# Modulation vectors with the float32 weight block as stationary operand and two conditioning columns streaming

## The chip, the core and the metric

The kernel runs on one core of a Trainium2 chip: TensorE (PE, with its weight loads PEld), VectorE (DVE), ScalarE (ACT), GpSimd (POOL) and SyncE (SP, which issues the DMAs here). The metric is the time of the kernel on the device in microseconds.

## The reference

One inference step of a backbone of two layers on 128 context tokens and 512 latent tokens, D = 1024. Each layer normalises its input, modulates it, sends it through one wide projection into three mixers (attention A, latent attention B, a bidirectional scan C), gates and merges them, and adds the result back. What the change touches is the modulation: for each of two conditioning vectors (`c_ctx` for context tokens, `c` for latent tokens) and each layer, a product of a vector of 1024 with a 1024 x 3072 matrix, split into shift, scale and gate.

```python
def _modulation(cond, w, b):
    m = jax.nn.silu(cond) @ w + b
    return jnp.split(m, 3, axis=-1)

shift, scale, gate = _modulation(c_ctx[None, None, :], w_mod[l], b_mod[l])
h = _rmsnorm(xp, norm_w[l]) * (1.0 + scale) + shift
out, ak, av, ckv, kr, s_f, s_b = _context_mixer(h, lp)
xp = xp + gate * out
```

The latent tokens go the same way with `c`.

## The kernel before

Features lie on partitions: the state is 8 tiles (`KT`) of 128 features x 640 tokens. Its modulated form `hh`, `hl` is a float32r pair (rounded part and remainder), and so is every weight block: `load_w1` fetches a block of 128 output columns (8 x 128 x 128, 512 KB, in `self.pieces` pieces), ACT rounds a piece into `whi` (L174), DVE or POOL subtracts it for `wlo` (L175), and three products (`hh` by `whi`, `hl` by `whi`, `hh` by `wlo`, L225 to L227, tile `pcm`) stand for one float32 product, in two halves of 320 tokens.

The modulations are 24 blocks of 128 outputs a layer. A block gives a column of 128 values for each of the two conditioning vectors in `modc`.

The first 16 (shift and scale of layer 0) are computed in the opening, by `modulation_first`, from float32 weights as they come (`wraw`, eight buffers): `sc2` (128 x 2, the two conditioning vectors) is stationary, the weights stream, the result is two rows of 128, which ACT copies (`mrow`, L263) and a second small product (L264) turns into two columns of 128. The opening also loads `x0`, sums its squares (`pss`, L311), spreads the reciprocal root over partitions (`prb`, L319), normalises (L326) and modulates into `hh`, `hl` (L163, L164). The first products that read them are the LoRA products (`plo`, L178 to L180, 96 of them), at the start of the scan stage.

The other 32 (8 gates of layer 0, 16 shift and scale blocks of layer 1, 8 gates of layer 1) lie in the scan stages as fillers. There a stream of projections (`c_inproj`, `spill`, `gate`), a Python generator, is played between the steps of the scan (`c_scan`: `sca`, `scb`), `pump(rate)` taking so many `yield`s from it, and after every `every` units `fillers` inserts a modulation. A scheduler with a timeline of its own then settles each engine's order. In these stages `pieces` is 2, and there are two raw buffers (`nraw`, of half a block each) and two `whi` and `wlo` buffers (`nw`), shared by projections and modulations. `modulation` (L241) uses the pair: `sc_t` (128 x 4, also split) is stationary, `whi` and `wlo` stream (L247, L248, 16 products), ACT copies four rows into the zeroed `mrow` (L249), and after a `yield` a float32 product with `mrow` as stationary operand and `sel` streaming (L251) sums and transposes them. The subtraction is given to POOL (`self.G`). The PSUM tile `pmod` comes from the two banks that the projections use.

Of the kernel before, what the change touches and what calls it, by code (L numbers as in the profile page):

```python
# [10 lines left out]
F32 = mybir.dt.float32  # L11
F32R = mybir.dt.float32r
AF = mybir.ActivationFunctionType
ALU = mybir.AluOpType
# [6 lines left out]
KT = 8  # L21
# [44 lines left out]
NR0 = 8  # L66
# [27 lines left out]
def f32(ap):  # L94
    return ap.bitcast(F32)
# [12 lines left out]
class Trunk:  # L108
    def __init__(self, ctx, tc, I, O):
# [5 lines left out]
        V, G = self.V, self.G  # L115
# [3 lines left out]
        self.dr = ctx.enter_context(tc.tile_pool(name="dr", bufs=1, space=DRAM))  # L119


        c = cst.tile([128, 202], F32, tag="small", name="small")
        nc.sync.dma_start(out=c, in_=I["small"])
        self.cT = c[:, 0:16].rearrange("p (k c) -> p k c", c=2)
        self.bmod = c[:, 16:64].rearrange("p (l k) -> p l k", l=DEPTH)
        self.fnw = c[:, 64:72]
        self.ident = c[:, 72:200]
        self.sel = c[:, 200:202]
        self.mrow = cst.tile([128, 128], F32, tag="mrow", name="mrow")
        G.memset(self.mrow, 0.0)  # L130

        self.bones_r = cst.tile([128, 128], F32R, tag="bones", name="bones")
        self.bones = f32(self.bones_r)
        for h in range(2):
            for g in range(2):
# [5 lines left out]
        self.sc2 = sc = cst.tile([128, KT, 2], F32, tag="sc", name="sc")  # L141
        self.S.activation(out=sc, in_=self.cT, func=AF.Tanh, scale=0.5)
        V.scalar_tensor_tensor(out=sc, in0=sc, scalar=1.0, in1=self.cT, op0=ALU.add, op1=ALU.mult)

        self.sc_t = st = cst.tile([128, 2, KT, 4], F32R, tag="sc_t", name="sc_t")
        self.S.mul(out=st[:, 0, :, 0:2], in_=sc, mul=0.5)
        V.scalar_tensor_tensor(out=st[:, 0, :, 2:4], in0=sc, scalar=0.5, in1=f32(st[:, 0, :, 0:2]),
                               op0=ALU.mult, op1=ALU.subtract)
        self.S.copy(out=st[:, 1, :, 0:2], in_=f32(st[:, 0, :, 0:2]))
        self.S.mul(out=st[:, 1, :, 2:4], in_=sc, mul=0.0)  # L150
        dr = self.dr
        self.x1 = dr.tile([KT, 128, T], F32, tag="x1", name="x1")
        self.gsp = [[dr.tile([128, T], F32, tag=f"gsp{b}_{k}", name=f"gsp{b}_{k}") for k in range(KT)] for b in range(3)]
# [84 lines left out]
        return r  # L238


    def modulation(self, l, ct, wp, ps, sub=None, tag="f"):  # L241

        PE, S = self.PE, self.S
        hi, lo = self.load_w1(wp, self.I["wmod"][l, ct], sub=sub)
        pm = ps.tile([128, 512], F32, tag=tag, name="pmod")
        for kt in range(KT):
            PE.matmul(pm[0:4, 0:128], lhsT=self.sc_t[:, 0, kt, :], rhs=hi[:, kt], start=(kt == 0), stop=False)  # L247
            PE.matmul(pm[0:4, 0:128], lhsT=self.sc_t[:, 1, kt, :], rhs=lo[:, kt], start=False, stop=(kt == KT - 1))  # L248
        S.copy(out=self.mrow[0:4], in_=pm[0:4, 0:128])  # L249
        yield  # L250
        PE.matmul(pm[:, 256:258], lhsT=self.mrow, rhs=self.sel, start=True, stop=True)  # L251
        self.V.tensor_scalar(out=self.modc[l][:, ct // KT, ct % KT, :], in0=pm[:, 256:258],  # L252
                             scalar1=self.bmod[:, l, ct:ct + 1], scalar2=None, op0=ALU.add)

    def modulation_first(self, ct, wp, ps, tag):

        raw = wp.tile([128, KT, 128], F32, tag="wr", name="wraw", bufs=NR0)
        self.nc.sync.dma_start(out=raw, in_=self.I["wmod"][0, ct])
        pm = ps.tile([128, 512], F32, tag=tag, name="pmod")
        for kt in range(KT):  # L260
            self.PE.matmul(pm[0:2, 0:128], lhsT=self.sc2[:, kt], rhs=raw[:, kt], start=(kt == 0), stop=(kt == KT - 1))
        row = wp.tile([4, 128], F32, tag="mrow", name="mrow", bufs=2)
        self.S.copy(out=row[0:2], in_=pm[0:2, 0:128])  # L263
        self.PE.matmul(pm[:, 256:258], lhsT=row[0:2], rhs=self.sel[0:2], start=True, stop=True)  # L264
        self.V.tensor_scalar(out=self.modc[0][:, ct // KT, ct % KT, :], in0=pm[:, 256:258], scalar1=0.5,
                             scalar2=self.bmod[:, 0, ct:ct + 1], op0=ALU.mult, op1=ALU.add)


    def layer_vectors(self, l):
# [1066 lines left out]
    def run(self):  # L1336
# [30 lines left out]
        ps = P("psA0", **PSA)  # L1367
        with ExitStack() as ctx:
            wp = pool(ctx, "wp0", 1, side="right")
            op = pool(ctx, "op0", 2, side="right")  # L1370
            xs = op.tile([128, KT, T], F32, tag="xs", name="xs", bufs=1)
            order = [(kt, ct, "g" if kt % 2 else "f") for kt in range(KT) for ct in (kt, KT + kt)]

            for kt, ct, tag in order[:MF]:
                self.modulation_first(ct, wp, ps, tag)
            self.layer_vectors(0)
            for kt in range(KT):
                nc.sync.dma_start(out=xs[:, kt], in_=self.I["x0"][kt])
                self.square(xs[:, kt], kt, op)
            for kt, ct, tag in order[MF:MG]:  # L1380
                self.modulation_first(ct, wp, ps, tag)
            self.normalise(xs, self.token_rstd(self.acc, self.sq, op, ps))
            for kt in range(KT):
                for k, ct, tag in order[MG:]:
                    if k == kt:
                        self.modulation_first(ct, wp, ps, tag)
                self.mod_vectors(0, [kt])
                self.modulate(0, xs, kt, 0, T, op)
        for l in range(DEPTH):
            plan = self.plan = NS(**PLAN[l])  # L1390
            if l:
                ps = P(f"psA{l}", **PSA)
            with ExitStack() as ctx, ExitStack() as ctx_c, ExitStack() as ctx_e:
                wp = pool(ctx, f"wp1{l}", 1)
                st = pool(ctx, f"st1{l}", 2)
# [18 lines left out]
                def fillers(n):  # L1414
                    for _ in range(n):
                        yield from units.pop(0)
                        count[0] += 1
                        while mods and count[0] >= every:
                            count[0] -= every
                            yield from self.modulation(*mods.pop(0), wp, ps, self.G)  # L1420

                def keys(p):

# [15 lines left out]
                def period(p, x):  # L1439

                    z = self.spill(self.silu2, l, W_CZ + p, wp, st, ps, self.zsp[p])
                    if p < 3:
                        def between():
                            yield from z
                            yield from fillers(plan.fb[p])
                        e = yield from prepare(*x, between())
                        yield from fillers(plan.share[p + 1] - plan.fb[p])
                        return e, (yield from keys(p + 2)) if p < 2 else None
                    yield from z
                    yield from fillers(plan.at[0])  # L1450
                    es = yield from self.attention_start(l, pools, wp, st, ps, lambda i: fillers(min(plan.at[i], len(units))))
                    yield from fillers(len(units))
                    for m in mods:
                        yield from self.modulation(*m, wp, ps, self.G)
                    return None, es

                c = self.play(prepare(*self.play(keys(0))))
# [77 lines left out]
def _layout(i):  # L1535
# [22 lines left out]
    def pc(v):  # L1558
# [14 lines left out]
    wo = np.stack([a["w_oa"], a["w_ob"], a["w_oc"]], 1)  # L1573
    r["wo"] = wo.reshape(2, 3, 4, 128, 4, 256).transpose(0, 1, 4, 3, 2, 5)
    r["wout"] = blocks1(a["w_out"])
    sel = np.zeros((128, 2), np.float32)
    sel[0:4] = np.concatenate([np.eye(2), np.eye(2)], 0)
    r["small"] = np.concatenate([
        np.stack([a["c_ctx"], a["c"][0]], -1).reshape(KT, 128, 2).transpose(1, 0, 2).reshape(128, 16),
        a["b_mod"].reshape(2, 24, 128).transpose(2, 0, 1).reshape(128, 48),  # L1580
        a["final_norm_w"].reshape(KT, 128).T, np.eye(128, dtype=np.float32), sel], 1)
    r["kc"] = a["cache_a_k"][0]
    r["vc"] = a["cache_a_v"][0]
    r["ckvc"] = a["cache_b_ckv"][0]
# [35 lines left out]
```

## Time and profile before

| | |
|---|---|
| median of 3 runs | 2349.75 us (2346.33 to 2349.75) |
| the profiled execution | 2358.59 us |
| its span, first to last instruction | 2356.9 us |
| mean granted TensorE clock | 0.934 |
| opening | 0 to about 61 us |
| scan stage of layer 0 | about 52 to 800 us |
| the 32 later modulations, first to last | 104.7 to 1909.3 us |

Busy shares are of the span. The clock is the share of the full 2.4 GHz that was granted; it has two levels, 1.00 and 0.50. A wait is the idle time of an engine before an instruction, with what ended it.

### The profile page before, as it was taken

Reading aid. Unit: us, or ns where it says so; the run is one execution under the profiler, and the core shown is the slowest. Engines: PE = TensorE matmul, PEld = TensorE weight load, DVE = VectorE, ACT = ScalarE, POOL = GpSimd, SP = SyncE. Lnnn points to the kernel's source line nnn. Section 1 sums busy time; section 2 is a strip of 40 time slices with the busy share of each in tenths; the row PEclk is TensorE's granted clock in tenths of the full one; section 3 lists DMA queues with packets and bytes.
Section 4 is the critical chain, followed back from the end, with each engine's and each line's share of the span. In section 5 each row is a group of like instructions: output and inputs, shape, how many; then the busy total and the mean of one; then the engine's idle time right before and its main releaser. Section 6 shows DMA issues by size and latency. Waiting matters only on the chain. (4 is left out here: it accounts for less than half of the span.)

```text
span 2356.9 us, 40407 instructions
## 1 busy us (share of the span) xinstructions
PE 2144.3 (91%) x15380; PEld 2025.6 (86%) x15380; DVE 1603.2 (68%) x3054; ACT 1107.0 (47%) x2462; POOL 694.8 (29%) x769
## 2 busy tenths in 40 slices
PE   8889998999779889999989999999897888999998
PEld 6889998989678777879988999989896877788898
DVE  4667878868544677775748778687774458677673
ACT  4544443444343567662344444443442436677333
POOL 3332536145233311102033143351632341210021
PEclk9999998999789899999989999999996989999999
DMA  6232222222223311125622322222222220110552
GB/s 224 77 100 80 82 75 81 86 90 94 79 75 98 107 36 52 39 76 172 203 64 68 106 73 86 74 71 84 81 82 76 73 95 30 51 46 17 186 183 89
DMA packets 111762, 209.70 MB, mean 89 GB/s; under 512 B 14416, under 2 KB 33488, under 8 KB 111568
## 3 DMA queue, kind: packets, MB, share of 16 engines
q1 hardware_dynamic: 111568, 207.12, 27.6%
q8 instruction: 121, 1.98, 0.3%
q14 instruction: 73, 0.60, 0.1%
HBM read 163.52 MB, written 43.55 MB: 88 GB/s over the span
## 5 line engine op out<-in xcount | busy, mean ns | idle before, releaser
L225 PE MATMUL pcm<-hh,whi 128*128 128x320 f32 x1952 | 636.1, 326 | 16.5 <-ACT xv L378 2.9
L227 PE MATMUL pcm<-hh,wlo 128*128 128x320 f32 x1952 | 627.9, 322 | 11.3 <-DVE wlo L175 11.3
L226 PE MATMUL pcm<-hl,whi 128*128 128x320 f32 x1952 | 625.1, 320 | 0.0
L225 PEld LDWEIGHTS pcm<-hh,whi 128*128 128x128 f32 x1952 | 382.1, 196 | 24.5 <-DVE modc L252 5.0
L227 PEld LDWEIGHTS pcm<-hh,wlo 128*128 128x128 f32 x1952 | 380.9, 195 | 15.1 <-DVE wlo L175 13.9
L226 PEld LDWEIGHTS pcm<-hl,whi 128*128 128x128 f32 x1952 | 381.9, 196 | 1.2
L174 ACT CAST whi<-wraw 128x512 fp32r<-128x512 f32 (+1 forms) x356 | 226.9, 666 | 322.0 <-PE pcm L226 116.8
L175 DVE TENSOR_TENSOR wlo<-wraw,whi 128x512 fp32r<-128x512 f32 (+1 forms) x262 | 220.9, 857 | 78.3 <-ACT whi L174 74.9
L175 POOL TENSOR_TENSOR wlo<-wraw,whi 128x512 fp32r<-128x512 f32 x94 | 124.4, 1337 | 157.4 <-ACT whi L174 152.4
L778 POOL COPY ubd<-VZ 64x128 f32<-64x128 f32 x160 | 65.0, 406 | 354.9 <-ACT VZ L775 324.3
L164 DVE TENSOR_TENSOR pl<-pp,ph 128x512 fp32r<-128x512 f32 x160 | 107.9, 684 | 35.5 <-ACT ph L163 34.7
L958 DVE TENSOR_REDUCE nm<-sc 128x1 f32<-128x640 f32 x128 | 104.2, 818 | 28.7 <-PE sc L955 27.5
L178 PE MATMUL pm<-yh,whi 128*128 128x320 f32 x384 | 121.5, 317 | 2.0 <-DVE OT L992 1.5
L179 PE MATMUL pm<-yl,whi 128*128 128x320 f32 x384 | 121.1, 315 | 0.5 <-DVE yl L167 0.4
L180 PE MATMUL pm<-yh,wlo 128*128 128x320 f32 x384 | 120.8, 315 | 0.7 <-DVE wlo L175 0.7
L163 ACT CAST ph<-pp 128x512 fp32r<-128x512 f32 x160 | 92.1, 585 | 46.5 <-PE pp L970 36.6
L960 ACT ACTIVATE P<-sc,nm 128x640 f32<-128x640 f32 x128 | 101.9, 797 | 17.4 <-DVE nm L958 14.0
L970 PE MATMUL pp<-small,P 128*128 128x128 f32 x640 | 102.0, 284 | 7.3 <-DVE pl L164 2.5
L767 PE MATMUL sca<-VZ,L 128*128 128x64 f32 x640 | 96.5, 296 | 11.1 <-DVE VZ L799 11.1
L767 PEld LDWEIGHTS sca<-VZ,L 128*128 128x128 f32 x640 | 93.8, 217 | 12.8 <-DVE VZ L799 12.3
L970 PEld LDWEIGHTS pp<-small,P 128*128 128x128 f32 x640 | 81.9, 146 | 25.0 <-DVE OT L992 3.9
L613 PE MATMUL pA<-L,BK 128*128 128x128 f32 x640 | 93.1, 290 | 6.3 <-DVE BK L549 3.1
(375 smaller groups left out, 4987.5 us busy)
## 6 DMA issues: line engine op xcount, KB each, us to landing
wraw<-in_win SPq DMA_DIRECT2D x156, 256.0 KB, 3.0
wraw<-in_wg SPq DMA_DIRECT2D x96, 256.0 KB, 3.0
wraw<-in_wmod SPq DMA_DIRECT2D x64, 256.0 KB, 3.1
gsp<-gt SPq DMA_DIRECT2D x48, 320.0 KB, 2.6
gt<-gsp SPq DMA_DIRECT2D x48, 320.0 KB, 3.5
wraw<-in_wo SPq DMA_DIRECT2D x24, 512.0 KB, 4.4
cm<-gsl SPq DMA_DIRECT2D x26, 320.0 KB, 2.7
wraw<-in_wmod SPq DMA_DIRECT2D x16, 512.0 KB, 6.6
```

The lines of the kernel that those rows point to most:

```text
L164: self.V.tensor_tensor(out=lo, in0=src, in1=f32(hi), op=ALU.subtract)
L174: self.S.copy(out=hi[part], in_=raw)
L175: sub.tensor_tensor(out=lo[part], in0=raw, in1=f32(hi[part]), op=ALU.subtract)
L178: self.PE.matmul(out, lhsT=lh, rhs=rh, start=first, stop=False)
L179: self.PE.matmul(out, lhsT=lh, rhs=rl, start=False, stop=False)
L180: self.PE.matmul(out, lhsT=ll, rhs=rh, start=False, stop=last)
L225: PE.matmul(p[0:m, 0:H], lhsT=wh[:, kt], rhs=self.hh[:, kt, rs], start=(kt == 0), stop=False)
L226: PE.matmul(p[0:m, 0:H], lhsT=wh[:, kt], rhs=self.hl[:, kt, rs], start=False, stop=False)
L227: PE.matmul(p[0:m, 0:H], lhsT=wl[:, kt], rhs=self.hh[:, kt, rs], start=False, stop=(kt == KT - 1))
L767: PE.matmul(a4[:, d, h], lhsT=L1[h][:, uu[d]].rearrange("p a s -> p (a s)"), rhs=VZ[h][:, cc[d], :], start=(h == 0 and d == 0), stop=False ...
L958: V.tensor_reduce(out=nm, in_=sc[:, :, 0:H], axis=AX.XY, op=ALU.max, negate=True)
L970: PE.transpose(p[:, qt * 128:(qt + 1) * 128], Ps[qt][:, t * 128:(t + 1) * 128], ident)
```

## The change

One method, `modulation`, replaces both. It streams the two columns of `sc2` against the raw float32 weights as stationary operand: 8 products per block, each of 128 x 128 by 128 x 2, straight into two columns of `pmod`, and DVE adds the bias with a factor 0.5. The rounding, the subtraction, the second stationary operand `sc_t`, the copied row and the second product are gone, with `sel` and `mrow`. There is a `yield` after each piece (two a modulation in the scan stages, before one). The raw buffers are read by PE itself.

```diff
-        self.sel = c[:, 200:202]
-        self.mrow = cst.tile([128, 128], F32, tag="mrow", name="mrow")
-        G.memset(self.mrow, 0.0)
...
-        self.sc_t = st = cst.tile([128, 2, KT, 4], F32R, tag="sc_t", name="sc_t")
-        self.S.mul(out=st[:, 0, :, 0:2], in_=sc, mul=0.5)
-        V.scalar_tensor_tensor(out=st[:, 0, :, 2:4], in0=sc, scalar=0.5, in1=f32(st[:, 0, :, 0:2]),
-                               op0=ALU.mult, op1=ALU.subtract)
-        self.S.copy(out=st[:, 1, :, 0:2], in_=f32(st[:, 0, :, 0:2]))
-        self.S.mul(out=st[:, 1, :, 2:4], in_=sc, mul=0.0)
...
-    def modulation(self, l, ct, wp, ps, sub=None, tag="f"):
-
-        PE, S = self.PE, self.S
-        hi, lo = self.load_w1(wp, self.I["wmod"][l, ct], sub=sub)
+    def modulation(self, l, ct, wp, ps, tag="f"):
+
         pm = ps.tile([128, 512], F32, tag=tag, name="pmod")
-        for kt in range(KT):
-            PE.matmul(pm[0:4, 0:128], lhsT=self.sc_t[:, 0, kt, :], rhs=hi[:, kt], start=(kt == 0), stop=False)
-            PE.matmul(pm[0:4, 0:128], lhsT=self.sc_t[:, 1, kt, :], rhs=lo[:, kt], start=False, stop=(kt == KT - 1))
-        S.copy(out=self.mrow[0:4], in_=pm[0:4, 0:128])
-        yield
-        PE.matmul(pm[:, 256:258], lhsT=self.mrow, rhs=self.sel, start=True, stop=True)
-        self.V.tensor_scalar(out=self.modc[l][:, ct // KT, ct % KT, :], in0=pm[:, 256:258],
-                             scalar1=self.bmod[:, l, ct:ct + 1], scalar2=None, op0=ALU.add)
-
-    def modulation_first(self, ct, wp, ps, tag):
-
-        raw = wp.tile([128, KT, 128], F32, tag="wr", name="wraw", bufs=NR0)
-        self.nc.sync.dma_start(out=raw, in_=self.I["wmod"][0, ct])
-        pm = ps.tile([128, 512], F32, tag=tag, name="pmod")
-        for kt in range(KT):
-            self.PE.matmul(pm[0:2, 0:128], lhsT=self.sc2[:, kt], rhs=raw[:, kt], start=(kt == 0), stop=(kt == KT - 1))
-        row = wp.tile([4, 128], F32, tag="mrow", name="mrow", bufs=2)
-        self.S.copy(out=row[0:2], in_=pm[0:2, 0:128])
-        self.PE.matmul(pm[:, 256:258], lhsT=row[0:2], rhs=self.sel[0:2], start=True, stop=True)
-        self.V.tensor_scalar(out=self.modc[0][:, ct // KT, ct % KT, :], in0=pm[:, 256:258], scalar1=0.5,
-                             scalar2=self.bmod[:, 0, ct:ct + 1], op0=ALU.mult, op1=ALU.add)
+        n = KT // self.pieces
+        for i in range(0, KT, n):
+            raw = wp.tile([128, n, 128], F32, tag="wr", name="wraw", bufs=self.nraw)
+            self.nc.sync.dma_start(out=raw, in_=self.I["wmod"][l, ct][:, i:i + n])
+            for k in range(n):
+                self.PE.matmul(pm[:, 0:2], lhsT=raw[:, k], rhs=self.sc2[:, i + k], start=(i + k == 0),
+                               stop=(i + k == KT - 1))
+            yield
+        self.V.tensor_scalar(out=self.modc[l][:, ct // KT, ct % KT, :], in0=pm[:, 0:2], scalar1=0.5,
+                             scalar2=self.bmod[:, l, ct:ct + 1], op0=ALU.mult, op1=ALU.add)
...
+            self.pieces, self.nraw = 1, NR0
...
-                self.modulation_first(ct, wp, ps, tag)
+                self.play(self.modulation(0, ct, wp, ps, tag))
...
-                            yield from self.modulation(*mods.pop(0), wp, ps, self.G)
+                            yield from self.modulation(*mods.pop(0), wp, ps)
```

The built order of PE in the opening, before: the products of a modulation (L261) and the product with its row (L264).

```order
L261 MATMUL pmod<-wraw,sc 2x128 x19
L264 MATMUL pmod<-small,mrow 128x2
L261 MATMUL pmod<-wraw,sc 2x128 x8
L264 MATMUL pmod<-small,mrow 128x2
L261 MATMUL pmod<-wraw,sc 2x128 x8
```

And after, from the start to the first LoRA products.

```order
L239 MATMUL pmod<-sc,wraw 128x2 x82
L288 MATMUL pss<-ones,acc 128x2 x5
L239 MATMUL pmod<-sc,wraw 128x2 x13
L296 MATMUL prb<-small,tr5b 128x128 x5
L239 MATMUL pmod<-sc,wraw 128x2 x33
L168 MATMUL plo<-hh,whi 128x320
L169 MATMUL plo<-hl,whi 128x320
```

All 128 products of the 16 modulations now stand ahead of the LoRA products, with nothing between them but `pss` and `prb`; before, the last of them and the LoRA products alternated.

SP's queue around one modulation of layer 0, before, with the semaphores that each DMA waits for (`DMAHW` of DMAs, `DVE_49` and `Pool_49` of those engines, `PE_49` of TensorE). `wraw` from `in_wmod` is the modulation's weight, from `in_wg` that of the gate block after it.

```order
L173 DMA wraw_7253<-in_wmod 128x512 [waits DMAHW7_49,DMAHW2_49,DVE_49]
L173 DMA wraw_7257<-in_wmod 128x512 [waits DMAHW3_49,DMAHW1_49,DVE_49]
L1253 DMA gsp0_7_95<-gt_7057 128x640 [waits DMAHW4_49,Activation_49]
L173 DMA wraw_7351<-in_wg 128x512 [waits DMAHW5_49,DMAHW2_49,Pool_49]
L173 DMA wraw_7355<-in_wg 128x512 [waits DMAHW6_49,DMAHW3_49,Pool_49]
```

And after, around one.

```order
L237 DMA wraw_7409<-in_wmod 128x512 [waits DMAHW7_49,DVE_49]
L237 DMA wraw_7419<-in_wmod 128x512 [waits DMAHW0_49,DVE_49]
L1230 DMA gsp1_4_93<-gt_7348 128x640 [waits DMAHW3_49,Activation_49]
L163 DMA wraw_7428<-in_wg 128x512 [waits DMAHW4_49,DMAHW1_49,PE_49]
L163 DMA wraw_7432<-in_wg 128x512 [waits DMAHW5_49,DMAHW2_49,PE_49]
```

What releases the next block's buffer has moved from POOL's subtraction to PE's products.

PE's order at the same modulation, after: the end of the gate before it, its own products from the two pieces, and the first products of the gate behind it.

```order
L217 MATMUL pcm_7381<-hh_149,wlo_7339 128x320
L239 MATMUL pmod_7408<-sc_77,wraw_7409 128x2 [waits DMAHW1_49,Activation_49]
L239 MATMUL pmod_7408<-sc_77,wraw_7409 128x2 x3
L239 MATMUL pmod_7408<-sc_77,wraw_7419 128x2 [waits DMAHW2_49]
L239 MATMUL pmod_7408<-sc_77,wraw_7419 128x2 x3
L215 MATMUL pcm_7437<-hh_149,whi_7426 128x320 [waits Activation_49]
```

Here four products of the second piece are all that stands between the first piece's release and the next block, whose `whi_7426` is cast from `wraw_7428`.

## Rows read from the trace of the kernel before

**Rows 1.** The page, part 1: busy us (share) and instructions.
```profile
PE 2144.3 (91%) x15380; PEld 2025.6 (86%) x15380; DVE 1603.2 (68%) x3054; ACT 1107.0 (47%) x2462; POOL 694.8 (29%) x769
```

**Rows 2.** Table by stretch: length, busy us of each engine (instructions), clock, DMA share, GB/s.
```profile
0.00:30.00 30.00, 23.10 (x181) 16.49 (x182) 8.07 (x25) 10.70 (x25) 7.61 (x19) 1.00 0.94 347
```

**Rows 3.** PE's waits, 52 to 850 us: us in total, times, longest.
```profile
PE pmod L248 <- POOL wlo L175: 2.1, 2, 1.7
PE pmod L251 <- ACT mrow L249: 1.9, 2, 1.3
...
PE pcm L225 <- DVE modc L252: 1.6, 1, 1.6
```

**Rows 4.** The modulation's own products in a stretch; PE's timeline around a second product.
```profile
509.50:510.80 1.30, 1.12 (x16) 0.96 (x16) 0.00 (x0) 0.00 (x0) 1.00 0.00 0
...
116.74 0.28 PE L251 MATMUL pmod<-small,mrow 128*128 128x2 f32 x2
...
117.11 0.31 PE L226 MATMUL pcm<-hl,whi 128*128 128x320 f32 x1
```

**Rows 5.** PE's timeline: neighbouring stream products at full clock, then at half.
```profile
60.98 0.31 PE L179 MATMUL plo<-hl,whi 128*128 128x320 f32 x1
61.13 0.31 PE L180 MATMUL plo<-hh,wlo 128*128 128x320 f32 x1
...
113.17 0.47 PE L226 MATMUL pcm<-hl,whi 128*128 128x320 f32 x1
113.43 0.47 PE L227 MATMUL pcm<-hh,wlo 128*128 128x320 f32 x1
```

**Rows 6.** Two columns on a stationary 128*128 block: full clock, durations of one, half clock.
```profile
29.66 1.28 PE L311 MATMUL pss<-ones,acc 128*128 128x2 f32 x10 [1.28 <-DVE acc L308]
...
L311 PE MATMUL pss<-ones,acc x30: 165/251/374, 29.7 to 2346.0; 128*128 128x2 f32 x30
...
1211.38 1.01 PE L311 MATMUL pss<-ones,acc 128*128 128x2 f32 x4 [3.60 <-POOL acc L300]
```

**Rows 7.** Table by stretch, as rows 2: the start, before and after three falls; L681 from 1490.1.
```profile
5.50:8.70 3.20, 3.17 (x16) 1.94 (x17) 0.00 (x0) 0.00 (x0) 0.00 (x0) 1.00 1.01 398
...
1490.10:1493.50 3.40, 3.40 (x75) 3.35 (x72) 1.61 (x4) 0.00 (x0) 0.00 (x0) 1.00 0.79 249
1493.60:1496.90 3.30, 3.30 (x14) 3.30 (x14) 0.28 (x1) 1.52 (x4) 0.58 (x2) 0.50 0.01 3
1503.80:1507.10 3.30, 2.47 (x23) 2.33 (x22) 2.13 (x6) 1.58 (x4) 2.95 (x2) 1.00 0.60 216
1507.20:1514.00 6.80, 5.43 (x22) 5.03 (x21) 3.33 (x8) 3.65 (x12) 5.01 (x6) 0.50 0.23 84
...
510.50:513.90 3.40, 2.00 (x15) 1.73 (x13) 2.59 (x6) 0.85 (x3) 0.78 (x1) 1.00 0.27 104
513.90:517.30 3.40, 3.40 (x15) 3.40 (x14) 2.49 (x3) 1.97 (x3) 1.28 (x1) 0.50 0.42 149
...
L681 PE MATMUL px<-NF,AB 32*32 32x32 f32 x75 | 3.7, 228 | 0.0
```

**Rows 8.** DVE's timeline at the opening's end; POOL's in layer 0's last group norm.
```profile
55.60 1.56 DVE L164 TENSOR_TENSOR hl<-mt,hh 128x640 fp32r<-128x640 f32 x2 [2.62 <-ACT hh L163]
...
771.64 1.30 POOL L175 TENSOR_TENSOR wlo<-wraw,whi 128x512 fp32r<-128x512 f32 x1 [1.17 <-ACT whi L174]
772.89 1.97 POOL L237 TENSOR_TENSOR gsb<-gs,nhalf 128x10 f32<-128x10 f32 x1
```

**Rows 9.** DMA issues (page, part 6), and timelines of SP, ACT and PE.
```profile
wraw<-in_win SPq DMA_DIRECT2D x156, 256.0 KB, 3.0
...
495.62 1.56 SPq L173 DMA_DIRECT2D wraw<-in_wg  x2
...
61.34 1.14 ACT L174 CAST whi<-wraw 128x512 fp32r<-128x512 f32 x2
...
62.01 0.42 PE L225 MATMUL pcm<-hh,whi 128*128 128x320 f32 x1 [0.57 <-ACT whi L174]
...
511.29 0.42 PE L225 MATMUL pcm<-hh,whi 128*128 128x320 f32 x1 [0.58 <-ACT gt L1252]
```

More of the change, by code (lines that the diff above doesn't have):

```diff
@@ L119, in __init__ @@
         self.dr = ctx.enter_context(tc.tile_pool(name="dr", bufs=1, space=DRAM))
-        c = cst.tile([128, 202], F32, tag="small", name="small")
+        c = cst.tile([128, 200], F32, tag="small", name="small")
         nc.sync.dma_start(out=c, in_=I["small"])
@@ L1380, in run @@
             for kt, ct, tag in order[MF:MG]:
-                self.modulation_first(ct, wp, ps, tag)
+                self.play(self.modulation(0, ct, wp, ps, tag))
             self.normalise(xs, self.token_rstd(self.acc, self.sq, op, ps))
@@ L1385, in run @@
                     if k == kt:
-                        self.modulation_first(ct, wp, ps, tag)
+                        self.play(self.modulation(0, ct, wp, ps, tag))
                 self.mod_vectors(0, [kt])
@@ L1453, in period @@
                     for m in mods:
-                        yield from self.modulation(*m, wp, ps, self.G)
+                        yield from self.modulation(*m, wp, ps)
                     return None, es
@@ L1575, in _layout @@
     r["wout"] = blocks1(a["w_out"])
-    sel = np.zeros((128, 2), np.float32)
-    sel[0:4] = np.concatenate([np.eye(2), np.eye(2)], 0)
     r["small"] = np.concatenate([
@@ L1580, in _layout @@
         a["b_mod"].reshape(2, 24, 128).transpose(2, 0, 1).reshape(128, 48),
-        a["final_norm_w"].reshape(KT, 128).T, np.eye(128, dtype=np.float32), sel], 1)
+        a["final_norm_w"].reshape(KT, 128).T, np.eye(128, dtype=np.float32)], 1)
     r["kc"] = a["cache_a_k"][0]
```

## The prediction

> **What bounds the kernel now.** I read the page's busy shares first, then a table by stage, then the list of PE's waits, then the instructions of the modulations alone. TensorE is busy 91% of the span [rows 1]; only in the opening 30 us are the DMA engines the fuller ones, at 0.94 [rows 2]. In the list of PE's waits in the scan stage of layer 0 (52 to 850 us) those on modulations come to 5.6 us: `wlo` from POOL 2.1, `mrow` from ACT 1.9, `modc` 1.6 [rows 3]. So PE time is time of the kernel there; ACT and POOL work is not, unless it holds PE up.
>
> **PE work of the 32 later modulations.** Now: 16 products in float32r take 1.12 us, the last of them some 0.22 after its start, so 60 ns each, 0.96 together [rows 4]. The product with the copied row is two passes: from the first of them (116.74) to the second stream matmul after it (117.11) 0.37 us pass, of which the stream matmul has 0.147 [rows 4, 5], so 0.22. Together 1.18 us. After: 8 float32 products of a 128*128 stationary block with two columns. The trace has this form as L311: ten passes (five matmuls) in 1.28 us, the last one 0.25 long, so 0.112 a pass [rows 6]. That is 16 x 0.112 = 1.79 us, 0.61 more, **+19.5 us** for 32. The Trainium skill (TensorE: Matmul & The Clock Gate, Back-to-back issue gap) gives about 25 ns as the floor for so few columns; by that alone a modulation would take 0.4 us, and this term would be -25 in place of +19.5. The rows decide against it.
>
> **The opening.** Its 16 modulations already use float32 without a split; only the roles change. PE starts at half speed (16 passes in the 3.2 us to 8.7, though the clock column, whose records begin there, reads 1.00) and goes on at full speed (181 by 30 us) [rows 2, 7]. With two streaming columns I expect it to stay at half. What speaks for that: before each fall in rows 7 PE was busy, 3.40 of 3.40 us from 1490.1 with 32*32 matmuls alone, 2.47 of 3.30 from 1503.8 with weight loads for 2.33; the clock then stood at 0.50 (1.2 GHz). At half clock a pass of this form takes 0.213 (four passes in 1.01, the last 0.37 long) [rows 6]. The order puts 82 products ahead of the sums of squares (`pss`): 82 x 0.426 = 34.9, so `pss` starts at 5.5 + 34.9 = 40.4 instead of 29.66. Then `pss` 2.1, 13 products 5.5, `prb` 2.1, 33 products 14.1: the first LoRA product at 64.2, all 96 of them after it (96 x 0.147 = 14.1) done at 78.3. They are done at 61.4 now [rows 5]: **+17**, all of it on the path, since the scan stage's stream starts behind them. If the clock rises instead, the opening is DMA's as before, and the last `hl` (57.2 now [rows 8]) plus its 12 products (1.8) would end the LoRA at 59: -2.5. I take +17.
>
> **The wait that the change adds.** Both raw pieces of a modulation are released by PE now, not by ACT and POOL. There are two raw buffers, so the next block's first piece can't be requested before the modulation's first four products have run, and SP's queue stands behind that wait with its spills. Before, the piece was requested long ahead: in the example of rows 9 both pieces at 495.62, for products that start at 511.29, just behind a modulation. After, from the fourth product to the next block's first: 0.25 for the product [rows 6], 3.0 for the DMA, 0.57 for the cast, and some 0.4 of hand-overs (my estimate: the first cast from 61.34 ends at 61.91, and PE goes on at 62.01, 0.1; with SP and its queue four such): 4.2 us [rows 9]. Against that stands what the order leaves PE in between, priced by rows 4 to 6. In 4 of the 32 places it is the other four products alone (0.9 us), in 16 some 1.3 to 3.4 us of scan and pair matmuls (mean 2.3), in 12 over 4 us. Sum: 4 x 3.3 + 16 x 1.9 + 0 = 44 us of bare PE. Low end 0: the scan's matmuls wait for DVE and ACT as it is, and their chain goes on in these gaps. I take **+25**, a little over half.
>
> **Clock in the scan stage.** A bare stretch next to 1.8 us of two-column products is what rows 7 show before the falls: from 510.5, where a modulation ends and PE then waits, it was busy 2.00 of 3.40 us, and the next 3.40 us were at 0.50. A spell of 3.4 us of stream costs 3.4 x (1 - 0.147/0.267) = 1.5 us [rows 5]. Ends: none, and one for each modulation, 48 us. I take 8 more: **+12**.
>
> **What it gives back.** ACT loses two casts (0.57 each) and a copy a modulation, POOL two subtractions of 1.3 us [rows 8, 9]. PE's waits on them go, 5.6 us. In the last group norm of a layer the power on POOL stands behind such a subtraction (it starts at 772.89, when the `wlo` of 771.64 is done [rows 8]): up to 1.3 us, twice. **-8**; at best, with shorter queues for the scan's copies too, -30. The bank that held `pmod` from the products over copy and second product is freed sooner; what hid that is the same stream, so I count nothing for it.
>
> **Sum.** 19.5 + 17 + 25 + 12 - 8 = +65.5 us. The profiled execution took 2358.59 us (span 2356.9), so 2424 there; the median of the runs shown is 2349.75, 8.8 less, and the forecast is 2349.75 + 65.5 = **2415 us**, 2.8% slower.
>
> **Rivals.** (a) *The clock stays up*: two-column products count as work for it. For: the opening now rises to full speed on modulations alone. Against: rows 7. Then 19.5 - 2.5 + 25 - 8 = +34, 2384 us. The Trainium skill (TensorE: Matmul & The Clock Gate, Part 1: The HAM clock gate) says that the gate goes by how busy the PE has been, and a PE full of weight loads and products is busy; by that rule this rival holds. The busy stretches before the falls in rows 7 speak against it. (b) *Faster*: the scan's matmuls cover the new wait, the longer products fall into PE's present waits, and only the relief of ACT and POOL is left. It decides if PE has 4.2 us of ready work behind the fourth product at nearly all places; the order gives that at 12 of 32. Price: -2.5 - 8 = -10.5, 2339; with a part of the longer products still to be seen, within 0.2% of 2350. (c) *The wait at full price*: the bare 44 us, and 15 spells at 1.5: 19.5 + 17 + 44 + 22 - 8 = +95, 2445. That the change doesn't do what it says is no rival: the order shows the products gone and the weights stationary.
>
> **How the numbers follow.** Forecast 0.5, (c) 0.18, (a) 0.18, (b) 0.14, of which 0.09 is faster by over 0.2% (about what a measurement of this kernel can tell from no change) and 0.05 within it. The range leaves out (b) below, and above it reaches past (c) by the uncertainty of the spells: 2356 to 2455. Faster 0.09, same 0.05, slower 0.86.
>
> **What would show each step.** Passes of `pmod` 0.112 apart at full clock, 0.21 at half. In the table by stage 0:30 at clock 0.5, `pss` near 40 us and the first stream matmul of the scan stage near 79. In PE's waits new ones, `pcm` on ACT's `whi` and behind that on the DMA of `wraw`, 1 to 3 us each. Mean clock under 0.92. I am wrong if `pss` stands near 30, if `pcm` waits no more on `whi` than now, or if `pn` and `sca` chains got so much shorter that PE's sum of waits fell.

## The result and the profile after

The changed kernel takes 2385.59 us (median of four runs, 2382.2 to 2389.29) against 2349.75: 1.0156 times as long, with a 95% interval of 1.0135 to 1.0176, so 36 us slower. Measured once more beside other runs it was 1.0155 (1.013 to 1.018). The forecast was 2415 us, 65 us slower: sign and range held, the size was nearly twice too large. To compare runs that were timed at different hours, every result below is given as its ratio to the kernel before on the same chip, and as that ratio times 2349.75 us. Ratios leave out one execution of the run with own raw buffers and one of the run with 128 columns in the opening, in which a much lower clock was granted (0.878 and 0.636).

The profiled execution took 2382.2 us (span 2380.5). It is the quickest of its kernel's four, while the profiled execution before (2358.59 us) is 8.8 us above its median, so the two profiles lie 24 us apart where the medians lie 36 apart: a difference between the two profiles, in the clock above all, is likely too small. Against [rows 1], TensorE is busy 34 us more at the same share, POOL 87 us less and ACT 35 us less:

```profile
PE 2178.0 (91%) x15284; PEld 2075.8 (87%) x15284; DVE 1577.1 (66%) x3053; ACT 1072.3 (45%) x2347; POOL 607.8 (26%) x704
```

**The opening.** TensorE's timeline from the start (start, us, line, operation, tiles, count; a float32 product is two passes):

```profile
5.31 35.12 PE L239 MATMUL pmod<-sc,wraw 128*128 128x2 f32 x164 [5.31 <-DMA wraw<-in_wmod]
40.29 2.27 PE L288 MATMUL pss<-ones,acc 128*128 128x2 f32 x10
42.43 5.69 PE L239 MATMUL pmod<-sc,wraw 128*128 128x2 f32 x26
47.97 2.48 PE L296 MATMUL prb<-small,tr5b 128*128 128x128 f32 x10
50.25 14.08 PE L239 MATMUL pmod<-sc,wraw 128*128 128x2 f32 x66
64.19 0.61 PE L168 MATMUL plo<-hh,whi 128*128 128x320 f32 x1
...
79.49 0.31 PE L170 MATMUL plo<-hh,wlo 128*128 128x320 f32 x1
```

164 passes from 5.31 to 40.29 are 0.213 us each, without a gap: the price of the half clock in [rows 6]. (The clock column reads 1.00 here as it did in [rows 7]: the clock records of this trace begin only at 67.0 us, and what lies before them counts as 1.00.) `pss` starts at 40.29, foreseen 40.4; the first LoRA product at 64.19, foreseen 64.2; the last ends at 79.8, foreseen 78.3. In [rows 5] it ended at 61.4, so the opening alone is 18.4 us longer. The LoRA's own products begin at half clock too:

```profile
66.73 0.46 PE L168 MATMUL plo<-hh,whi 128*128 128x320 f32 x1
67.00 0.34 PE L169 MATMUL plo<-hl,whi 128*128 128x320 f32 x1
67.17 0.30 PE L170 MATMUL plo<-hh,wlo 128*128 128x320 f32 x1
67.32 0.31 PE L168 MATMUL plo<-hh,whi 128*128 128x320 f32 x1
```

They come 0.27 apart up to 67.00 and 0.15 to 0.17 apart behind it: the clock rose there, 62 us into the work.

**The scan stage's waits.** PE's waits from 52 to 850 us, the same view as [rows 3] (total, times, longest), after:

```profile
PE pcm L215 <- ACT whi L164: 22.5, 13, 3.2
...
PE scb L750 <- DVE wbd L747: 4.7, 4, 1.6
PE pcm L217 <- DVE wlo L165: 4.1, 4, 2.7
PE pyt L817 <- POOL YY L812: 4.0, 1, 4.0
```

and more rows of that list for the kernel before:

```profile
PE pyt L840 <- POOL YY L835: 14.8, 2, 13.4
PE scb L773 <- DVE wbd L770: 9.0, 6, 2.7
PE pcm L227 <- DVE wlo L175: 6.5, 8, 1.7
...
PE px L681 <- DVE NF L672: 3.6, 3, 1.9
```

The new wait is there, at the size foreseen: 22.5 us in layer 0's scan stage, and by the page's group of the line (busy, mean ns, idle before) 24.4 in the whole run:

```profile
L215 PE MATMUL pcm<-hh,whi 128*128 128x320 f32 x1952 | 640.7, 329 | 34.9 <-ACT whi L164 24.4
```

But the old waits shrank as well, and by more.

**Both scan stages as sums.** For a table by stretch over the two scan stages (end of the LoRA products to the attention's first `sc` product, in either layer) these are the last lines: length, then TensorE's busy time. First of before, all instructions, then those of `pcm` and of `pmod` alone:

```profile
sum 1437.30, PE 1298.33 PEld 1255.21 DVE 991.74 ACT 615.62 POOL 525.19; mean PE 649.16 PEld 627.61 DVE 495.87 ACT 307.81 POOL 262.60
```
```profile
sum 1437.30, PE 884.53; mean PE 442.27
```
```profile
sum 1437.30, PE 53.72; mean PE 26.86
```

The same three of after:

```profile
sum 1446.50, PE 1317.19 PEld 1279.74 DVE 969.06 ACT 581.65 POOL 435.38; mean PE 658.60 PEld 639.87 DVE 484.53 ACT 290.82 POOL 217.69
```
```profile
sum 1446.50, PE 894.68; mean PE 447.34
```
```profile
sum 1446.50, PE 60.77; mean PE 30.39
```

The stages are only 9 us longer in these two executions. TensorE's idle time (length less busy) went *down*, from 139.0 to 129.3, although 24 us of new waits lie in it. The modulations' products take 7 us more. The projections, the same 5184 `pcm` products, take 10 us more: laid over the trace's clock records, 101 us of their busy time lie in stretches at half clock, against 80 before. All stretches at half clock in the two stages together are no longer than before, though (235 us against 238).

**How the wait costs what it costs.** One place shows both effects. First the TensorE timeline at the end of layer 0's scan stage, after:

```profile
788.98 1.84 PE L239 MATMUL pmod<-sc,wraw 128*128 128x2 f32 x16
794.06 0.64 PE L215 MATMUL pcm<-hh,whi 128*128 128x320 f32 x1 [3.24 <-ACT whi L164]
```

ACT and SP at the same place:

```profile
790.07 6.94 SPq L163 DMA_DIRECT2D wraw<-in_wg  x4
```
```profile
793.39 1.21 ACT L164 CAST whi<-wraw 128x512 fp32r<-128x512 f32 x2 [3.77 <-DMA wraw<-in_wg]
```

The 16 passes start at 788.98, the next block's DMA is issued at 790.07, ACT has waited for it until 793.39, PE until 794.06. That is the chain the prediction drew. What follows is the second bill: the table by stretch (as [rows 2]) shows the wait and then 3.4 us at half clock.

```profile
789.00:792.40 3.40, 1.82 (x17) 1.73 (x16) 2.15 (x13) 0.44 (x1) 1.95 (x1) 1.00 0.55 180
792.40:794.00 1.60, 0.00 (x0) 0.00 (x0) 0.69 (x1) 0.61 (x2) 0.77 (x1) 1.00 0.42 151
794.00:797.40 3.40, 3.34 (x11) 3.06 (x12) 2.62 (x3) 0.59 (x2) 0.77 (x1) 0.51 0.26 72
797.40:800.80 3.40, 3.40 (x24) 3.40 (x24) 1.08 (x2) 1.24 (x2) 0.00 (x0) 0.99 0.30 96
```

11 products in 3.4 us at clock 0.51, 24 in the next 3.4 us: 13 fewer, at 0.147 us each some 1.9 us lost behind a wait of 3.24.

**Where a wait is given back.** The longest wait of the stage before was `pyt` on POOL in a group norm, with nothing to run for 13.38 us:

```profile
640.04 1.11 PE L786 MATMUL sca<-ubd,AB 128*128 128x128 f32 x4 [0.50 <-POOL ubd L778]
654.53 1.76 PE L840 MATMUL pyt<-small,YY 128*128 128x128 f32 x7 [13.38 <-POOL YY L835]
```

After, the stream is late there, and a modulation and 48 projection products (from 664.53, rows left out) stand in that gap:

```profile
659.98 1.84 PE L239 MATMUL pmod<-sc,wraw 128*128 128x2 f32 x16
661.68 0.69 PE L763 MATMUL sca<-ubd,AB 128*128 128x128 f32 x4
...
678.33 2.39 PE L817 MATMUL pyt<-small,YY 128*128 128x128 f32 x10 [3.98 <-POOL YY L812]
```

So at this one place 9.4 us come back (13.38 to 3.98), and 10.8 in all of this stage's waits of `pyt` on POOL (14.8 to 4.0).

### The profile page after: what moved, and what is told of

The parts are those of the page before. It is cut to its first block, busy times and chain, and to the rows that moved or that the text cites. A ratio compares the mean times of both kernels' runs of the same rounds, so it can differ in the third digit from the quotient of the medians.

```text
span 2380.5 us, 39890 instructions
## 1 busy us (share of the span) xinstructions
PE 2178.0 (91%) x15284; PEld 2075.8 (87%) x15284; DVE 1577.1 (66%) x3053; ACT 1072.3 (45%) x2347; POOL 607.8 (26%) x704
## 5 line engine op out<-in xcount | busy, mean ns | idle before, releaser
L215 PE MATMUL pcm<-hh,whi 128*128 128x320 f32 x1952 | 640.7, 329 | 34.9 <-ACT whi L164 24.4
L164 ACT CAST whi<-wraw 128x512 fp32r<-128x512 f32 (+1 forms) x292 | 192.0, 677 | 285.9 <-DMA wraw<-in_win 66.7
L239 PEld LDWEIGHTS pmod<-sc,wraw 128*128 128x128 f32 x768 | 117.8, 239 | 7.3 <-issue 5.3
L239 PE MATMUL pmod<-sc,wraw 128*128 128x2 f32 x768 | 115.7, 279 | 6.3 <-DMA wraw<-in_wmod 5.3
L744 PE MATMUL sca<-VZ,L 128*128 128x64 f32 x640 | 94.4, 289 | 10.8 <-DVE VZ L776 8.1
L590 PEld LDWEIGHTS pA<-L,BK 128*128 128x128 f32 x640 | 89.0, 211 | 17.0 <-ACT AB L595 10.5
```

The lines of the kernel that those rows point to most:

```text
L164: self.S.copy(out=hi[part], in_=raw)
L215: PE.matmul(p[0:m, 0:H], lhsT=wh[:, kt], rhs=self.hh[:, kt, rs], start=(kt == 0), stop=False)
L239: self.PE.matmul(pm[:, 0:2], lhsT=raw[:, k], rhs=self.sc2[:, i + k], start=(i + k == 0), stop=(i + k == KT - 1))
L590: PE.matmul(pA[:, j * 128:(j + 1) * 128], lhsT=BK[:, u].rearrange("p a s -> p (a s)"), rhs=L1[h][:, u].rearrange("p a s -> p (a s)"), star ...
```

## The experiments

### The opening alone, both ways

The changed kernel with the old opening:

```diff
-                self.play(self.modulation(0, ct, wp, ps, tag))
+                self.modulation_first(ct, wp, ps, tag)
```

> The changed kernel, but its opening computes the first 16 modulations in the old way (two conditioning columns stationary, the weights stream); the 32 later ones stay in the new form. The opening theory (two-column products leave PE at half clock there, and the 18 us are on the path): the last LoRA product ends near 61.4 us instead of 79.8, and the median falls from 2385.6 by 18 to about 2367. Rival (the scan stage is paced by its own chain of scan steps and takes an earlier start back): the LoRA ends near 61 as well, but the median stays at 2381 to 2386.

Measured: 1.0040 (1.0021 to 1.0058), 9 us over the kernel before, so the old opening takes back 27 of 36 us. The last LoRA product ends at 62.0.

The kernel before with the new opening, the reverse edit:

> The kernel before, with only the opening in the new form; the 32 later modulations keep the split and the second product. The opening theory: the last LoRA product ends near 79.8 us and the median rises from 2349.75 by 18 to about 2368, so that this run and the one with the old opening split the 36 us in halves. Rival (taken back in the scan stage): 2350 to 2355.

Measured: 1.0112 (1.0087 to 1.0136), +26 us; the LoRA ends at 80.9. The rival is out both times: an opening that is 18 to 20 us longer is not taken back in the scan stage. It even costs 7 to 9 us more than its own stretch, which is little more than the intervals leave uncertain. Where those lie these runs don't settle: between the two profiles of the changed kernel alone, a stage behind differs by up to 5 us.

### The wait: raw buffers of its own

```diff
-            raw = wp.tile([128, n, 128], F32, tag="wr", name="wraw", bufs=self.nraw)
+            raw = wp.tile([128, n, 128], F32, tag="wr" if self.pieces == 1 else "wm", name="wraw", bufs=self.nraw)
```

> The changed kernel, with two raw buffers of their own for the later modulations, so that the next projection block's DMA waits for no modulation product. The wait theory: PE's waits of pcm on ACT's whi fall from 24.4 us to the 2 to 4 that the kernel before shows, and the median falls by about 20 to 2365. Rival (PE would wait there for the scan's chain all the same): the waits on whi fall as much, but those on scb, sca, pA or pyt rise, and the median stays within 5 us of 2386.

Measured: 1.0070 (1.0042 to 1.0098), +16 us, so 20 us of the 36 go. PE's waits, 52 to 850 us:

```profile
PE pyt L817 <- POOL YY L812: 14.9, 2, 13.3
PE scb L750 <- DVE wbd L747: 10.6, 10, 2.7
...
PE px L658 <- DVE NF L649: 5.0, 2, 3.9
```

`pcm` waits on `whi` no more, and, as the rival said, the old waits are back at their old size, `pyt` and `scb` above all. Yet the time fell as the theory said. The sums over both scan stages (all, then `pcm`) show where:

```profile
sum 1424.70, PE 1299.53 PEld 1265.10 DVE 968.12 ACT 576.13 POOL 445.71; mean PE 649.77 PEld 632.55 DVE 484.06 ACT 288.07 POOL 222.86
```
```profile
sum 1424.70, PE 869.23; mean PE 434.61
```

Idle time fell by 4 us only (125.2 against 129.3), the projections by 25 us (869.2 against 894.7), with 58 us of their busy time at half clock against 101. In this pair most of the wait's price is clock. That the projections are slower behind the wait holds in every run: with the new form and shared raw buffers `pcm` takes 893 to 897 us (three executions, the old opening and the second profile of the changed kernel among them), with own buffers 866 to 877 in seven, whatever else was changed in them (885 in the eighth, the one with the copy put back, below). That this is the wait's whole price does not, as the next pair shows.

Both edits together, old opening and own buffers:

> Both edits together: old opening, new form in the scan stages, own raw buffers there. If both theories hold and add, 2385.6 - 18 - 20 = 2347, at the time of the kernel before or 2 to 8 us under it; what is then left of the longer PE work (19.5 us) must have been paid for by the relief of ACT and POOL. If the wait's rival holds, 2367, as with the old opening alone.

Measured: 0.9966 (0.9952 to 0.9981), 8 us *under* the kernel before, and 17 us under the old opening alone. Opening and wait add within the noise: the opening costs 27 us with shared and 24 with own buffers, the wait 20 with the new and 17 with the old opening. The sums over both scan stages (all, then `pcm`), first with the old opening alone:

```profile
sum 1440.80, PE 1309.24 PEld 1273.47 DVE 969.88 ACT 581.82 POOL 430.76; mean PE 654.62 PEld 636.73 DVE 484.94 ACT 290.91 POOL 215.38
```
```profile
sum 1440.80, PE 892.88; mean PE 446.44
```

Then with own buffers as well:

```profile
sum 1427.40, PE 1304.03 PEld 1268.21 DVE 967.73 ACT 576.39 POOL 440.66; mean PE 652.01 PEld 634.11 DVE 483.87 ACT 288.19 POOL 220.33
```
```profile
sum 1427.40, PE 872.01; mean PE 436.01
```

Here the projections fell by 21 us, but idle time fell by 8 (131.6 to 123.4) and the rest of TensorE's busy time rose by 16. The stretches at half clock together are as long as before (218 and 221 us), and the mean granted clock over twelve executions each is 0.9415 and 0.9412. So the price of the wait, 17 to 20 us, is shown, but its split into idle time and clock is not: it differs between the two pairs.

So the new form of the 32 later modulations, freed of the wait, gains 8 us, where the prediction had it lose 23.5 (19.5 + 12 - 8). (That -8 of it is the prediction's relief; that the measured sum is -8 too is chance.)

### What the longer products cost

On that last kernel, with every second product of the later modulations left out (each modulation then is the sum over half of its inputs):

```diff
-                self.PE.matmul(pm[:, 0:2], lhsT=raw[:, k], rhs=self.sc2[:, i + k], start=(i + k == 0),
-                               stop=(i + k == KT - 1))
+                if k % 2 == 0:
+                    self.PE.matmul(pm[:, 0:2], lhsT=raw[:, k], rhs=self.sc2[:, i + k], start=(i + k == 0),
+                                   stop=(i + k == KT - 2))
```

> Old opening, new form with own raw buffers in the scan stages (2343.4 us), with every second product of the 32 later modulations left out (all their weights are still loaded). Theory of the prediction's first term (1.79 us a modulation, all on the path): half of it goes, 32 x 0.9 = 29 us, median 2315. Rival (the scan's chain sets the pace where the modulations lie, and products fall into time that PE would wait): 2335 to 2343.

Measured: 0.9904 (0.9881 to 0.9926), 15 us less, between the two: the products of the modulations are on the path for about half of their time (15 of 31 us, with an interval of 8 to 21). The sums over both scan stages (all, then `pcm`) of this run:

```profile
sum 1412.00, PE 1284.77 PEld 1249.99 DVE 967.30 ACT 574.47 POOL 448.89; mean PE 642.39 PEld 625.00 DVE 483.65 ACT 287.24 POOL 224.44
```
```profile
sum 1412.00, PE 876.50; mean PE 438.25
```

The busy time of `pmod` fell from 62.4 to 31.0 us, TensorE's whole busy time by 19 only (from 1304.0). Idle time rose by 4 (127.2 against 123.4) and the projections took 4.5 more.

### What the relief of ACT and POOL is worth

Still on the same kernel, the casts and subtractions put back with no reader, first into a scratch tile of their own:

```diff
+            if self.pieces == 2:
+                hi = wp.tile([128, n, 128], F32R, tag="xh", name="xhi", bufs=1)
+                self.S.copy(out=hi, in_=raw)
+                self.G.tensor_tensor(out=hi, in0=raw, in1=f32(hi), op=ALU.subtract)
```

> The same base (2343.4 us) with the old work of the other engines added again: ACT rounds each raw piece into a scratch tile of its own and POOL subtracts, and nobody reads what they write. TensorE's work and the projections' buffers are as in the base. Theory (what paid for the longer products is the relief of ACT and POOL as engines): the median rises by 20 or more, to 2363 or above, with PE's waits on wlo, gt, xlo or YY grown. Rival (the relief is that of the whi and wlo buffers, which the modulations no longer take from the projections): within 5 us of 2343.

Measured: 1.0005 (0.9988 to 1.0022), 9 us more than without. Then into the projections' `whi` and `wlo` buffers:

```diff
+        hi = wp.tile([128, KT, 128], F32R, tag="wh", name="xhi", bufs=self.nw)
+        lo = wp.tile([128, KT, 128], F32R, tag="wl", name="xlo", bufs=self.nw)
...
+            self.S.copy(out=hi[:, i:i + n], in_=raw)
+            self.G.tensor_tensor(out=lo[:, i:i + n], in0=raw, in1=f32(hi[:, i:i + n]), op=ALU.subtract)
```

> As the run before it, but ACT and POOL write into the whi and wlo buffers that the projections use, two of each, as in the kernel before. Theory (relief of the engines): the same as the run before it, 2363 or above. Rival (relief of the buffers): this one alone rises by 20 or so.

Measured: 1.0013 (0.9996 to 1.003), 11 us more. The two can't be told apart from each other, so the buffers matter little; the engines' relief is worth 9 to 11 us, half of what the theory asked for and close to the 8 of the prediction. Which waits it removes isn't shown: the theory's sign, longer waits of TensorE, is missing, for its idle time in the scan stages is 120.9 and 119.1 us with the casts put back and 123.4 without, each in one execution. The mean clock over the executions is lower (0.939 and 0.938 against 0.941).

Copy and second product put back, with the bank held meanwhile:

```diff
...
+        row = self.sm.tile([128, 2], F32, tag="mcol", name="mcol")
+        self.S.copy(out=row, in_=pm[:, 0:2])
+        yield
+        self.PE.matmul(pm[:, 256:258], lhsT=self.ident, rhs=row, start=True, stop=True)
...
```

> Old opening, new form with own raw buffers in the scan stages (0.9966 of the kernel before, 8 us under it), with a copy and a second product put back: ACT copies the two columns, and after a yield a float32 product with the identity as stationary operand puts them back into the same PSUM tile, so that the bank is held as long as in the kernel before. What the runs have not placed so far is some 13 us of the gain in the scan stages. Theory (the bank that pmod holds over copy and second product keeps the projections' next tile waiting): 10 to 20 us more, 2352 to 2362, a ratio of 1.001 or more. Rival (only the product itself is added, 32 times 0.22 us, at the half price that the run with half the products showed): 3 to 4 us more, a ratio of 0.998.

Measured: 0.9971 (0.9951 to 0.9991), 1 us more. The theory of the bank falls; the prediction had counted nothing for it.

### Are the extra buffers the gain?

The kernel before, with raw buffers of their own for its modulations and nothing else:

```diff
-            raw = pool.tile(list(src.shape), F32, tag="wr", name="wraw", bufs=self.nraw)
+            raw = pool.tile(list(src.shape), F32, tag=rt, name="wraw", bufs=self.nraw)
...
-        hi, lo = self.load_w1(wp, self.I["wmod"][l, ct], sub=sub)
+        hi, lo = self.load_w1(wp, self.I["wmod"][l, ct], sub=sub, rt="wm")
```

> The kernel before, untouched but for raw buffers of their own for the 32 later modulations. Theory (there the raw buffer was released early by ACT and POOL, so no wait goes): 2349 within 3 us, and the 8 us by which the new form with own buffers beats the kernel before belong to the new form. Rival (they belong to the extra buffers, whatever the form): 2341.

Measured: 1.0087 (1.0058 to 1.0115), 20 us slower, which neither expected. The buffers alone are no gain. With them the scheduler put the DMAs in another order, and with it every engine's. TensorE's idle time in the scan stages is the same (138.7 against 139.0); the mean granted clock over its executions was 0.936, against 0.943 for the kernel before beside it. Among the executions of the kernel before, 0.001 of mean clock went with 1.1 to 1.7 us, so the clock is, by this estimate, some 7 to 12 of the 20 us. The rest stays open, and so does whether the new order is the cause.

### The clock in the opening

The changed kernel with own raw buffers; in the opening 128 columns stream against each block, 126 of them zeros:

```diff
+            self.scw = wp.tile([128, KT, 128], F32, tag="scw", name="scw")
+            self.G.memset(self.scw, 0.0)
+            self.V.tensor_copy(out=self.scw[:, :, 0:2], in_=self.sc2)
...
+                w, sc = (128, self.scw) if self.pieces == 1 else (2, self.sc2)
+                self.PE.matmul(pm[:, 0:w], lhsT=raw[:, k], rhs=sc[:, i + k], start=(i + k == 0),
+                               stop=(i + k == KT - 1))
```

> The changed kernel with own raw buffers (2362.1 us), but in the opening 128 columns stream against each weight block, the two conditioning columns and 126 of zeros, so that TensorE has the same weight loads and products, only longer streams. Theory (with two-column products the clock stays at half, with wide ones it rises): pmod passes go from 0.213 to about 0.112 us or to the pace of the DMA after the first microseconds, pss starts near 30, the last LoRA product ends near 61.4, and the median falls by 19 to about 2343. Rival (the clock stays at half in any product whose time is its weight load): pss stays near 40, the LoRA's end near 80, the median at 2362.

Measured: 0.9928 (0.9901 to 0.9956), 17 us under the kernel before and 33 under the same kernel with two columns. TensorE's timeline:

```profile
5.74 18.52 PE L240 MATMUL pmod<-scw,wraw 128*128 128x128 f32 x144 [5.74 <-DMA wraw<-in_wmod]
...
27.93 1.25 PE L289 MATMUL pss<-ones,acc 128*128 128x2 f32 x10 [0.90 <-DVE acc L286]
...
34.36 7.41 PE L240 MATMUL pmod<-scw,wraw 128*128 128x128 f32 x64 [0.38 <-DVE rbt L299]
...
59.22 0.31 PE L170 MATMUL plo<-hh,wlo 128*128 128x320 f32 x1
```

The same weight loads, in nearly the same order: 64 passes in 7.41 us are 0.116 each where they were 0.213, `pss` starts at 27.93 and the LoRA ends at 59.5, earlier than in [rows 5]. With 64 times the columns the passes are faster, so their time was not their streaming; the clock changed. The gain is more than the 19 us expected: the opening's own stretch gives 21.8 of the 33 (its LoRA ended at 81.3), and where the other 11 lie, a little more than the two intervals leave uncertain, isn't settled.

Then 64 columns in the scan stages' modulations as well:

```diff
-                w, sc = (128, self.scw) if self.pieces == 1 else (2, self.sc2)
+                w, sc = (128, self.scw) if self.pieces == 1 else (64, self.scx)
...
+            self.scx = self.cst.tile([128, KT, 64], F32, tag="scx", name="scx")
+            self.V.tensor_copy(out=self.scx, in_=self.scw[:, :, 0:64])
```

> The run with 128 columns streaming in the opening (2335 us), and now 64 columns, 62 of them zeros, in the 32 later modulations too. Theory of the clock term (two-column products beside waits bring spells of half clock): the mean granted clock rises from 0.941 by 0.003 or more, and by the spread within one kernel's executions (0.001 of clock goes with 1.0 to 1.7 us) the median falls by 3 to 6 us to 2330. Rival (the spells come from the waits of the scan whatever the modulations do): clock and median stay, 2335 within 3.

Measured: 0.9914 (0.9889 to 0.9938), 20 us under the kernel before, the fastest of those that leave no product out. The mean clock over its executions is 0.946 against 0.943 of the kernel before beside it, as the theory has it (with 128 columns in the opening alone, both had 0.943). The two ratios lie within each other's intervals, so that these columns gain time isn't shown.

The changed kernel once more, beside these:

> The changed kernel once more, beside the two runs after it, for a median from more executions. Both theories expect 2386 within 4 us; where it is nearer to 2378, the opening (22 us in the kernel before) and the wait (12 us with the old opening, 23 with the new one) simply add, and the 36 us of the first comparison were high.

Measured: 1.0155 (1.013 to 1.018), +36 us. Its median, 2381.2, is lower, but so was that of the kernel before beside it (2345.2); by ratios the 36 us stand.

## Why the prediction was right in sign and wrong in size

| term | forecast | measured |
|---|---|---|
| opening | +17 | +24 to +27; its own stretch +18.4 |
| the new wait | +25 | +17 to +20, clock included |
| PE work of 32 modulations | +19.5 | +7 in busy time, about half of it on the path, so some +4 |
| clock in the scan stages | +12 | `pcm` +10 in the profiles, no more half clock in all; what it costs lies in the wait's price |
| gives back | -8 | -9 to -11 by the casts put back; old waits: see the fifth point |
| the last three together, once the wait is gone | +23.5 | -8 |
| all | +65.5 | +36 |

By this table the sum is too high by 17 to 20 us at wait and clock and by some 15 at the PE work, and too low by 7 to 10 at the opening.

**The opening: right**, to 1.5 us at every point of its timeline. Rival (a), the clock that stays up, is out, though its sum (2384 us) came nearest to the time: it had the opening at -2.5. Rival (b) is out with the opening and the wait that the runs show, and (c) with 24.4 us of waits where it took 44. TensorE's first row in the timeline after is 35 us without a gap at 0.213 a pass, the half clock. The Trainium skill (TensorE: Matmul & The Clock Gate, Part 1: The HAM clock gate) says that the gate goes by how busy the PE has been; by "busy" as the profile counts it, the trace disagrees. With the same loads and 128 columns the clock rose.

**The wait: right in place and length, with another bill.** 24.4 us on `whi` over the whole run stand against the 25 of the sum; that 25 was picked as a little over half of 44, so its hit is partly luck. But TensorE's idle time didn't rise by them, and the projections behind them became slower. Own buffers took away 25 us of projections and 4 of idle time with the new opening, 21 and 8 with the old one; the rest of TensorE's busy time took 8 and 16 of it again. The prediction had split wait and clock into two terms and added both, +37; together they are 17 to 20.

**PE work: mis-sized.** The new form is as priced: 16 passes in 1.84 us with the last one's length, 1.79 in the sum. The old one was dearer than the 1.18 of [rows 4]: summed over both scan stages `pmod` took 53.7 us before, 1.68 a modulation, and 60.8 after, +7. Part of this is how busy time counts: the tail of a last product, beside which the next one runs already, is in it twice in the old form (1.12 and 0.28 in [rows 4]) and once in the new. And only about half counts, as the run with half of the products shows. Where the other half went, the waits show only in small part: idle time rose by 4 us there, and `pcm` and other products took 12 us more. The step that failed is "PE time is time of the kernel there".

**The clock in the scan stages: right at the places, not in the sum.** Half clock stands right behind the waits, as at 794, and the projections bear more of it, but the two stages together have no more half clock than before (235 us against 238). The stretch of [rows 7] from 510.5 that the term was drawn from stood behind a modulation of the old form, so it could show what a wait does, not what two columns do. The forecast of a mean under 0.92 was wrong and didn't follow from the term: the changed kernel's executions beside the kernel before had recorded means of 0.934 to 0.941, those of the kernel before 0.939 to 0.948. The recorded means of the changed kernel leave out the half clock of the opening, up to 67.0; with it the profiled execution would have some 0.925 in place of 0.939 (0.939 less half of 67/2380), still above 0.92.

**What it gives back: the old waits were missing.** The sum took -8 and named -30 as the best that could be. In the profiles idle time fell by 10 us with 24 us of new waits in it, so 34 came back: 10.8 at `pyt`, whose gap the delayed stream filled, and by layer 0's lists some 2 to 5 us each at `scb`, `px`, `wlo` and the modulations' own waits, the rest in small rows. The prediction listed only waits that name a modulation. That is why the new waits did not lengthen TensorE's idle time. Of the relief of ACT and POOL, 9 to 11 us are shown by the casts that were put back, the size that was forecast, but not by waits of TensorE, as the forecast had it.

What stays open: relief (-9 to -11) and half of the work (+4) make about -6 of the -8. But two more buffers, with the new order of instructions that came with them, moved the kernel before by 20 us for no reason that its waits show, and every edit of the scan stages brought a new order too. The price of the wait has the same sign and nearly the same size in two pairs, which speaks for the wait; the single terms are good to some 10 us, no better.

## What to carry to other kernels

Before the operands of a small product are swapped, look at who released the buffer: if an engine that ran ahead did and now TensorE does, the next block's load starts late, and a buffer of its own is the mend (17 to 20 us here). Read the spacing of passes where such products stand alone: at twice the full-clock spacing, streaming more columns against the same weights, zeros if need be, can cost nothing: it gave 33 us here, of which 22 in the opening itself. And before a new wait is added to a sum, look for old waits that the delayed work will fill.

## What was not expected of the hardware

TensorE without a gap for 35 us, and with hardly one for 59, stayed at half clock with two streaming columns, as the prediction expected; that it ran the same blocks at 0.116 us a pass with 128 columns was not in it. A wait of 3.24 us behind such products was followed by 3.4 us of projections at half clock, which lost some 1.9 us, more than half of the wait once more. And executions of one kernel differ by as much as 0.013 in mean clock (0.936 to 0.949, the kernel before) and 20 us in time, so an effect under 10 us needs many of them.

The Trainium skill (TensorE: Matmul & The Clock Gate, LDWEIGHTS) gives columns / 1.2 in ns for a weight load, by which 128 columns would take 107 ns, an estimate. The 0.112 to 0.116 us from pass to pass at full clock are near that; the 0.213 at half clock show that it is no constant.
